# Hybrid RWKV-7 / HGRN2 step: norm_g spread earlier and by two engines, last masks moved to VectorE, one weight fetch moved up

## The chip, the cores and the metric

One core of one Trainium2 chip runs the kernel. The metric is device time in microseconds of one execution; before the change the median of 3 runs is 1124.75 us (1123.86 to 1125.27).

## The reference

One layer of a decoder trunk for 256 prompt tokens and 64 sample tokens (8 sequences of 8), all float32. Cut to what matters:

```
h = rms_norm(x, norm_g)                       # x * rsqrt(mean(x^2) + eps) * norm_g
p = h @ w_in                                  # one projection, 2048 -> P_TOTAL columns
cur = p[..., :SHIFT_W]; sh = cur + (prev - cur) * shift_mu
y_a, s_a = rwkv7_recurrence(r, decay, k, v, kk, a, s_a)   # S = S diag(w) - (S kk)(kk a)^T + v k^T
o_b, s_b = gla_chunkwise(q_b, k_b, i_b, log_g, s_b)       # S = diag(g) S + k v^T
merged = sigmoid(p_ga) * (y_a @ proj_a) + sigmoid(p_gb) * (y_b @ proj_b)
y = x + merged @ w_out; then a final rms_norm
```

Outputs are y for both groups and the new states.

## The kernel before, in words

The 320 tokens stand as columns. h is kept transposed and split into two parts (hhi and hlo, 16 blocks of 128 features); each block of 1024x128 weights is fetched into one of three raw buffers, split into whi (a cast by ScalarE) and wlo (a subtraction), and each output tile of 128 columns takes 16 x 3 products on TensorE (whi with hhi, whi with hlo, wlo with hhi), 48 of 320 columns in a row. After the opening a recorder (L69 to L292) lists the operations of the eight head pairs and a planner with costs orders them; that part and all that follows are not touched by the change.

The opening (L376 to L673) has two parts. Up to L497 the order is the program's own: loads on the sync queue, clearings and selections on GpSimd. Behind L544 the order of TensorE, ScalarE, VectorE and GpSimd is the order in which the code is written, so each engine's queue is first in, first out as the text stands.

What the opening does, with names. norm_g arrives as gq, four rows of 512. To spread it over 128 partitions it is split into two parts in gr (L574, L575), and four products with a selector sel write it to gps, from where it is copied to gb (L577 to L579). squares (L499) sums x squared per token on ScalarE, scale (L504) turns that into a factor ssq, gain (L510) multiplies x (xt) by ssq and gb on VectorE, in six instructions ahead of the first low part. turn (L520) transposes on TensorE into tps, high and low (L527, L531) make hhi and hlo. warm(n) (L539) puts n dummy products wps on TensorE, whose results nobody reads. first (L608) is the first output tile (wd, ad; its columns start at 128*24), worked off in pieces of four blocks; half (L615) splits half a weight block, with GpSimd subtracting; divide(2, 1, G) and divide(0, 1, G) (L398, L657, L668) split a whole block with GpSimd subtracting. fetch (L394) loads a block; fetch(2, 1024, 1) at L669 writes the raw buffer that divide(2, 1, G) has read, so it waits for that subtraction.

On GpSimd stand, ahead of those subtractions, the masks: mk (the third of three pairs, L473 to L475, is a product with seqm) and mu8, four copies of mf as bytes (L493, L494). Behind the first tile the transposes cps and sps give cols and sst (L658 to L664), from which bounds (L679) and wd_ad (L1374) make neg, lbt and uQ; uQ becomes lora_a and lora_w, and the product called a in the profile (a<-lora_a,ast) is the first on TensorE that needs them.

Of the kernel before, what the change touches and what calls it, by code (L numbers as in the profile page):

```python
# [9 lines left out]
F32 = mybir.dt.float32  # L10
# [284 lines left out]
def hybrid_step(ctx, tc, x_prompt, x_sample, state_rwkv, state_hgrn, state_shift, norm_g, w_in,  # L295
# [4 lines left out]
    V, S, G, T = nc.vector, nc.scalar, nc.gpsimd, nc.tensor  # L300

    S.add_instruction(mybir.InstLoadActFuncSet(
        name=nc.get_next_instruction_name(), act_func_set_id=EXP_LN_SET, ins=[], outs=[]))
# [11 lines left out]
    def ctile(shape, name, dt=F32, pool=rconst):  # L315
        return pool.tile(shape, dt, name=name, tag=name)
# [59 lines left out]
    with tc.tile_pool(name="start", bufs=1) as st, \  # L376
            tc.tile_pool(name="pst", bufs=6, space=PSUM) as pst:
        gq = st.tile([4, 512], F32, name="gq")
        nc.sync.dma_start(gq, norm_g.rearrange("o (r c) -> (o r) c", c=512))
        gb = st.tile([128, D], F32, name="gb")  # L380
# [13 lines left out]
        def fetch(b_, c0, k8):  # L394
            nc.sync.dma_start(wraw[b_], win[1024 * k8:1024 * k8 + 1024, c0:c0 + 128]
                              .rearrange("(k p) c -> p k c", p=128))

        def divide(b_, n, sub):  # L398
            for j in range(n):
                ks = slice(8 * j // n, 8 * (j + 1) // n)  # L400
                S.copy(whi[b_][:, ks], wraw[b_][:, ks])
                sub.tensor_sub(wlo[b_][:, ks], wraw[b_][:, ks], whi[b_][:, ks].bitcast(F32))
            return whi[b_], wlo[b_]

        for k8 in range(2):
            fetch(k8, 128 * 24, k8)

        gr = st.tile([64, 512], F32R, name="gr")
        sel = st.tile([64, 4, 128], F32R, name="sel")
# [13 lines left out]
        for r0, t_ in ((W0, w0), (A0, a0), (KK_, k_k), (KA, k_a), (LW, ln_w), (LB, ln_b), (LG, lb_logits)):  # L423
# [3 lines left out]
        ssr = st.tile([100, 2, 128], F32, name="ssr")  # L427
        nc.sync.dma_start(ssr, state_shift[0].rearrange("s (r c) -> (s r) c", c=128)
                          .rearrange("(j q) c -> q j c", j=2))
        fetch(2, 0, 0)  # L430


        id64 = ctile([128, 64], "id64")
        G.tensor_add(id64, ident[:, 0:64], ident[:, 64:128])
# [1 line left out]
        def keep_ge(ap, pattern, base, cm, fill=0.0):  # L436
            G.affine_select(out=ap, in_=ap, pattern=pattern, compare_op=ALU.is_ge, fill=fill,
                            base=base, channel_multiplier=cm)
# [8 lines left out]
        seqm = ctile([128, NSEQ], "seqm")  # L447
# [19 lines left out]
        mk = ctile([128, 3, 2, 64], "mk")  # L467
        G.memset(mk[:, 0:2], 1.0)
        for c_ in range(2):
            for sl in HS:  # L470
                keep_ge(mk[sl, c_], [[1, 2], [1, 64]], -1, -1)
        blk = seqm[:, :, None].to_broadcast([128, 8, 8])
        for x in range(2):  # L473
            G.tensor_mul(mk[:, 2, x].rearrange("p (s i) -> p s i", i=8),
                         mk[:, 0, x].rearrange("p (s i) -> p s i", i=8), blk)  # L475


        mf = st.tile([32, 3, 32], F32, name="mf")
        mu8 = ctile([128, 3, 32], "mu8", U8)
        G.memset(mf, 1.0)  # L480
        for n, sz in enumerate((8, 8, 16)):
# [8 lines left out]
            G.memset(lv[:, :, 0, :], 0.0)  # L490
            keep_ge(lv[:, :, 1, :], [[-2 * sz, nb], [0, sz]], 0, 1)
            keep_ge(lv[:, :, 1, :], [[2 * sz, nb], [0, sz]], sz - 1, -1)
        for g in range(4):  # L493
            G.tensor_copy(mu8[32 * g:32 * g + 32], mf)  # L494

        junk = st.tile([128, D], F32, name="junk")
        ssq = [st.tile([128, 2], F32, name=f"ssq{j}") for j in range(3)]  # L497

# [40 lines left out]
        def warm(n):  # L539
            for _ in range(n):  # L540
                T.matmul(wps[:, :256], ones[:, :128], ones, start=True, stop=True)

        tps = {}
        with tc.manual_schedule(engines={mybir.EngineType.PE, mybir.EngineType.Activation, mybir.EngineType.DVE,  # L544
                                        mybir.EngineType.Pool}):
            ones = st.tile([128, 256], F32R, name="ones")
            V.memset(ones.bitcast(F32), 1.0)

            jr_sum, jr_mean, jr_cent, jr_all = (ctile([128, 128], n, F32R)
                                                for n in ("jr_sum", "jr_mean", "jr_cent", "jr_all"))  # L550
            V.memset(jr_all.bitcast(F32), 1.0 / 128.0)
            for t_, x in ((jr_sum, 1.0), (jr_mean, 1.0 / 64.0)):
                V.memset(t_.bitcast(F32), 0.0)
                for sl in HS:
                    V.memset(t_[sl, sl].bitcast(F32), x)
            V.tensor_sub(jr_cent, ident, jr_mean.bitcast(F32))

            yz = ctile([128, 2, 2, 2, 64], "yz")
            yd = ctile([128, 2, 2, 64], "yd")
            qz = ctile([128, NSEQ, 32], "qz")  # L560
            arp = ctile([128, 5, 2, 2, 64], "arp")
            for t_ in (yz, qz, lora_lw[HS[1]].bitcast(F32), lora_la[HS[0]].bitcast(F32)):
                V.memset(t_, 0.0)


            rs_a = ctile([128, NT], "rs_a")
            rs_b = ctile([128, NT], "rs_b")
            V.memset(rs_a, 1.0)
            V.memset(rs_a[:, 0:NP_:64], 0.0)
            V.memset(rs_a[:, NP_::8], 0.0)  # L570
            V.memset(rs_b, 1.0)
            V.memset(rs_b[:, ::8], 0.0)

            S.copy(gr[0:4], gq)  # L574
            V.tensor_sub(gr[32:36], gq, gr[0:4].bitcast(F32))  # L575
            for c_ in range(4):
                ps = pst.tile([128, 512], F32, name="gps", tag="t")  # L577
                T.matmul(ps, sel[:, c_], gr, start=True, stop=True)
                V.tensor_copy(gb[:, 512 * c_:512 * c_ + 512], ps)  # L579
            V.memset(arp, 0.0)  # L580
            warm(16)
            squares(2)
            scale(2)
            gain(2, 0, 2)
            turn(2, 0)
            warm(3)
            gain(2, 2, 2)
            turn(2, 1)
            warm(4)
            squares(0)  # L590
            scale(0)
            gain(0, 0, 2)
            turn(0, 0)
            turn(0, 1)
            squares(1)
            scale(1)
            gain(0, 2, 2)
            gain(1, 0)
            turn(1, 0)
            gain(1, 1)  # L600
            turn(1, 1)
            high(2, 0)
            high(0, 0)
            low(2, 0)
            low(0, 0)
            first_ps = psm.tile([128, 512], F32, name="mps", tag="m")

            def first(part, k4):  # L608

                w, x = ((whi, hhi), (whi, hlo), (wlo, hhi))[part]  # L610
                for k_ in range(4 * k4, 4 * k4 + 4):
                    T.matmul(first_ps[:, :NT], w[k4 // 2][:, k_ % 8], x[:, k_], start=part == 0 and k_ == 0,
                             stop=part == 2 and k_ == KT - 1)

            def half(b_, hf):  # L615

                ks = slice(4 * hf, 4 * hf + 4)
                S.copy(whi[b_][:, ks], wraw[b_][:, ks])
                G.tensor_sub(wlo[b_][:, ks], wraw[b_][:, ks], whi[b_][:, ks].bitcast(F32))

            half(0, 0)
            high(1, 0)
            low(1, 0)
            first(0, 0)
            gain(1, 2)
            gain(1, 3)
            half(0, 1)
            high(2, 1)
            high(0, 1)
            high(1, 1)  # L630
            low(2, 1)
            low(0, 1)
            low(1, 1)
            turn(0, 2)
            first(0, 1)
            turn(1, 2)
            first(1, 0)
            first(2, 0)
            half(1, 0)
            high(0, 2)  # L640
            high(1, 2)
            low(0, 2)
            low(1, 2)
            turn(0, 3)
            turn(1, 3)
            first(0, 2)
            first(1, 1)
            first(2, 1)
            half(1, 1)
            fetch(0, 0, 1)  # L650
            high(0, 3)
            high(1, 3)
            low(0, 3)
            low(1, 3)
            first(1, 2)
            first(2, 2)
            divide(2, 1, G)  # L657
            ps = pst.tile([128, 512], F32, name="cps", tag="t")  # L658
            T.transpose(ps[:, :128], rows, ident)
            V.tensor_copy(cols, ps[:, :106])  # L660
            ps = pst.tile([128, 512], F32, name="sps", tag="t")
            for j in range(2):
                T.transpose(ps[:, 100 * j:100 * j + 100], ssr[:, j], ident[:100, :100])
            V.tensor_copy(sst.rearrange("p s r -> p (s r)"), ps[:, :200])  # L664
            for part in range(3):
                first(part, 3)
            fetch(1, 1024, 0)
            divide(0, 1, G)  # L668
            fetch(2, 1024, 1)  # L669
            for j in range(4):  # L670
                S.copy(seq4[32 * j:32 * j + 32], seqm[0:32, 0:4])
            S.copy(lvz[HS[1], :, 1], lvs[low_])
            S.copy(lvz[low_, :, 0], lvs[low_])  # L673
# [766 lines left out]
    with tc.manual_schedule():  # L1440
# [3 lines left out]
        V, S, G, T, Y = (book.proxy(e) for e in ("V", "S", "G", "PE", "Y"))  # L1444
        record_all()
        V, S, G, T = real
# [27 lines left out]
    for m in range(KT):  # L1474
# [7 lines left out]
        ps = psf.tile([128, 512], F32, name="ppa", tag="f")  # L1482
# [3 lines left out]
        ps = psf.tile([128, 512], F32, name="ppb", tag="f")  # L1486
# [143 lines left out]
```

## Time and profile before

| what | us |
|---|---|
| median of 3 runs | 1124.75 (1123.86 to 1125.27) |
| profiled execution, its own time | 1124.7 |
| its span in the trace | 1122.0 |
| TensorE busy | 1102.9 (98%) |
| VectorE busy | 760.4 (68%) |
| ScalarE busy | 693.2 (62%) |
| GpSimd busy | 192.8 (17%) |

The names in the profile are PE for TensorE (PEld its weight loads), DVE for VectorE, ACT for ScalarE, POOL for GpSimd and SPq for the sync queue. A time of a row is counted from the span's start. In a timeline, a row is one instruction or several alike in a run; the bracket is the engine's idle time before it and what ended that. The ends of matmuls are modelled and reach into the next row, and spans on GpSimd are rough. The granted clock is 1.0 in every slice of the opening.

### The profile page before, as it was taken

What the parts mean: (1) busy time and instruction counts of PE and PEld (TensorE: products, weight loads), DVE (VectorE), ACT (ScalarE), POOL (GpSimd) and SP (SyncE); (2) the same over time, 40 slices, a digit from 0 to 9 for tenths busy, and PEclk for the clock granted to TensorE, in tenths of its full rate; (3) what the DMA queues carried; (4) which work ended last, traced back from release to release, by engine and by line L of the source; (5) the groups of instructions that cost most, each with busy time, mean ns of one, the idle gap of its engine ahead of it and who ended that gap; (6) DMA issues with size and microseconds to landing.
All of it is one profiled execution on the core that took longest, in us unless ns stands there. A gap on an engine that the chain in (4) does not pass through costs nothing.

```text
span 1122.0 us, 23659 instructions
## 1 busy us (share of the span) xinstructions
PE 1102.9 (98%) x9240; PEld 1066.5 (95%) x9240; DVE 760.4 (68%) x1618; ACT 693.2 (62%) x1572; POOL 192.8 (17%) x411
## 2 busy tenths in 40 slices
PE   6999999999999999999999999999999999999997
PEld 5999999999999999999999999999999999988886
DVE  8778888887887887887887876444444444437532
ACT  6777777677778678677776876444444444436322
POOL 9531231221311411412312200000000000000000
PEclk9999999999999999999999999999999999999999
DMA  6743545435435436435444354555555555587512
GB/s 177 202 130 107 152 118 146 136 100 157 125 96 158 131 105 165 133 106 159 117 132 137 101 142 142 147 151 150 149 151 150 150 150 149 151 256 267 173 35 93
DMA packets 283107, 159.87 MB, mean 142 GB/s; under 512 B 22893, under 2 KB 273264, under 8 KB 282356
## 3 DMA queue, kind: packets, MB, share of 16 engines
q1 hardware_dynamic: 282996, 158.37, 49.5%
q8 instruction: 72, 1.18, 0.5%
q14 instruction: 39, 0.32, 0.1%
HBM read 148.53 MB, written 9.81 MB: 141 GB/s over the span
## 4 chain that ended last, share of the span: by engine, by line
PE 94%; POOL 2%; ACT 2%; issue 1%; DVE 0%; DMA 0%; ACTq 0%; POOLq 0%; DVEq 0%
PE mps L1448 41%; PE a L1448 10%; PE mps L359 6%; PE mps L360 6%; PE mps L361 6%; PE b L1448 3%; PE po L1531 3%; PE po L1533 3%; PE po L1532 3%; PE ppa L359 2%; PE ppb L360 2%; PE ppb L359 2%; PE ppa L360 2%; PE ppb L361 2%; PE ppa L361 2%; PE y L1448 1%
## 5 line engine op out<-in xcount | busy, mean ns | idle before, releaser
L1448 PE MATMUL mps<-hhi,whi 128*128 128x320 f32 x1088 | 345.1, 317 | 0.0
L1448 PE MATMUL mps<-hlo,whi 128*128 128x320 f32 x1088 | 344.6, 317 | 0.0
L1448 PE MATMUL mps<-hhi,wlo 128*128 128x320 f32 x1088 | 344.1, 316 | 0.0
L1448 PEld LDWEIGHTS mps<-hhi,whi 128*128 128x128 f32 x1088 | 205.0, 188 | 3.6 <-issue 2.7
L1448 PEld LDWEIGHTS mps<-hlo,whi 128*128 128x128 f32 x1088 | 205.1, 188 | 1.1 <-issue 0.4
L1448 PEld LDWEIGHTS mps<-hhi,wlo 128*128 128x128 f32 x1088 | 205.0, 188 | 0.7
L349 ACT CAST whi<-raw 128x1024 fp32r<-128x1024 f32 x88 | 92.4, 1050 | 162.7 <-PE mps L360 107.3
L350 DVE TENSOR_TENSOR wlo<-raw,whi 128x1024 fp32r<-128x1024 f32 x88 | 107.8, 1226 | 124.9 <-ACT whi L349 124.8
L1448 DVE TENSOR_TENSOR wlo<-raw,whi 128x1024 fp32r<-128x1024 f32 x134 | 164.7, 1229 | 17.1 <-ACT whi L1448 15.9
L1448 ACT CAST whi<-raw 128x1024 fp32r<-128x1024 f32 x134 | 140.2, 1046 | 57.0 <-PE mps L1448 54.6
L361 PE MATMUL mps<-hhi,wlo 128*128 128x320 f32 x448 | 138.7, 310 | 0.0
L359 PE MATMUL mps<-hhi,whi 128*128 128x320 f32 x448 | 138.7, 310 | 0.0
L360 PE MATMUL mps<-hlo,whi 128*128 128x320 f32 x448 | 138.7, 309 | 0.0
L361 PEld LDWEIGHTS mps<-hhi,wlo 128*128 128x128 f32 x448 | 84.1, 188 | 0.0
L360 PEld LDWEIGHTS mps<-hlo,whi 128*128 128x128 f32 x448 | 84.1, 188 | 0.0
L359 PEld LDWEIGHTS mps<-hhi,whi 128*128 128x128 f32 x448 | 84.1, 188 | 0.0
L1520 DVE TENSOR_TENSOR wlo<-raw,whi 128x1024 fp32r<-128x1024 f32 x32 | 38.6, 1223 | 39.0 <-ACT whi L1519 38.9
L1519 ACT CAST whi<-raw 128x1024 fp32r<-128x1024 f32 x32 | 33.0, 1050 | 48.5 <-DMA raw<-in_w_out_dram 21.3
L1448 POOL TENSOR_TENSOR vm<-v,seq 96x512 fp32r<-96x512 f32 x16 | 16.9, 1054 | 200.1 <-ACT uK L1448 152.4
L1531 PE MATMUL po<-whi,mhi 128*128 128x512 f32 x128 | 50.1, 392 | 0.7 <-DVE gbt L1488 0.7
L1533 PE MATMUL po<-wlo,mhi 128*128 128x512 f32 x128 | 50.1, 391 | 0.0
L1532 PE MATMUL po<-whi,mlo 128*128 128x512 f32 x128 | 50.0, 391 | 0.0
(435 smaller groups left out, 2244.0 us busy)
## 6 DMA issues: line engine op xcount, KB each, us to landing
raw<-in_w_in_dram SPq DMA_DIRECT2D x194, 512.0 KB
raw<-in_w_out_dram SPq DMA_DIRECT2D x32, 512.0 KB
raw<-in_proj_a_dram SPq DMA_DIRECT2D x16, 512.0 KB
raw<-in_proj_b_dram SPq DMA_DIRECT2D x16, 512.0 KB
s<-in_state_hgrn_dram SPq DMA_DIRECT2D x8, 512.0 KB
out_dram<-s SPq DMA_DIRECT2D x8, 512.0 KB
s<-in_state_rwkv_dram SPq DMA_DIRECT2D x8, 256.0 KB
out_dram<-s SPq DMA_DIRECT2D x8, 256.0 KB
```

Of the source, the lines that this page charges most:

```text
L349: S.copy(hi[:, ks], raw[:, ks])
L350: sub.tensor_sub(lo[:, ks], raw[:, ks], hi[:, ks].bitcast(F32))
L359: T.matmul(dst, hi[:, q, :], xhi[:, k, :], start=(k == 0), stop=False)
L360: T.matmul(dst, hi[:, q, :], xlo[:, k, :], start=False, stop=False)
L361: T.matmul(dst, lo[:, q, :], xhi[:, k, :], start=False, stop=(k == nk - 1))
L1448: o.fn(*o.args, **o.kw)
L1519: S.copy(hi, raw)
L1520: V.tensor_sub(lo, raw, hi.bitcast(F32))
L1531: T.matmul(pt, h, hi, start=first, stop=False)
L1532: T.matmul(pt, l, hi, start=False, stop=False)
L1533: T.matmul(pt, h, lo, start=False, stop=end)
```

## The change

The split of norm_g and its four products move ahead of VectorE's clearings of yz, qz and the others; of the four copies to gb ScalarE makes the first and third. The dummy products ahead of the first transpose grow from 16 to 20. The product that makes the last pair of mk and the four copies of mu8 leave GpSimd and stand on VectorE behind divide(2, 1, G), ahead of the copy to cols. The fetch of the third weight block is issued ahead of the small loads.

```diff
--- before.py
+++ after.py
@@ -404,6 +404,7 @@
 
         for k8 in range(2):
             fetch(k8, 128 * 24, k8)
+        fetch(2, 0, 0)
 
         gr = st.tile([64, 512], F32R, name="gr")
         sel = st.tile([64, 4, 128], F32R, name="sel")
@@ -427,8 +428,6 @@
         ssr = st.tile([100, 2, 128], F32, name="ssr")
         nc.sync.dma_start(ssr, state_shift[0].rearrange("s (r c) -> (s r) c", c=128)
                           .rearrange("(j q) c -> q j c", j=2))
-        fetch(2, 0, 0)
-
 
         id64 = ctile([128, 64], "id64")
         G.tensor_add(id64, ident[:, 0:64], ident[:, 64:128])
@@ -469,10 +468,6 @@
         for c_ in range(2):
             for sl in HS:
                 keep_ge(mk[sl, c_], [[1, 2], [1, 64]], -1, -1)
-        blk = seqm[:, :, None].to_broadcast([128, 8, 8])
-        for x in range(2):
-            G.tensor_mul(mk[:, 2, x].rearrange("p (s i) -> p s i", i=8),
-                         mk[:, 0, x].rearrange("p (s i) -> p s i", i=8), blk)
 
 
         mf = st.tile([32, 3, 32], F32, name="mf")
@@ -490,9 +485,6 @@
             G.memset(lv[:, :, 0, :], 0.0)
             keep_ge(lv[:, :, 1, :], [[-2 * sz, nb], [0, sz]], 0, 1)
             keep_ge(lv[:, :, 1, :], [[2 * sz, nb], [0, sz]], sz - 1, -1)
-        for g in range(4):
-            G.tensor_copy(mu8[32 * g:32 * g + 32], mf)
-
         junk = st.tile([128, D], F32, name="junk")
         ssq = [st.tile([128, 2], F32, name=f"ssq{j}") for j in range(3)]
 
@@ -555,6 +547,13 @@
                     V.memset(t_[sl, sl].bitcast(F32), x)
             V.tensor_sub(jr_cent, ident, jr_mean.bitcast(F32))
 
+            S.copy(gr[0:4], gq)
+            V.tensor_sub(gr[32:36], gq, gr[0:4].bitcast(F32))
+            for c_ in range(4):
+                ps = pst.tile([128, 512], F32, name="gps", tag="t")
+                T.matmul(ps, sel[:, c_], gr, start=True, stop=True)
+                (V.tensor_copy if c_ % 2 else S.copy)(gb[:, 512 * c_:512 * c_ + 512], ps)
+
             yz = ctile([128, 2, 2, 2, 64], "yz")
             yd = ctile([128, 2, 2, 64], "yd")
             qz = ctile([128, NSEQ, 32], "qz")
@@ -570,15 +569,8 @@
             V.memset(rs_a[:, NP_::8], 0.0)
             V.memset(rs_b, 1.0)
             V.memset(rs_b[:, ::8], 0.0)
-
-            S.copy(gr[0:4], gq)
-            V.tensor_sub(gr[32:36], gq, gr[0:4].bitcast(F32))
-            for c_ in range(4):
-                ps = pst.tile([128, 512], F32, name="gps", tag="t")
-                T.matmul(ps, sel[:, c_], gr, start=True, stop=True)
-                V.tensor_copy(gb[:, 512 * c_:512 * c_ + 512], ps)
             V.memset(arp, 0.0)
-            warm(16)
+            warm(20)
             squares(2)
             scale(2)
             gain(2, 0, 2)
@@ -655,6 +647,12 @@
             first(1, 2)
             first(2, 2)
             divide(2, 1, G)
+            blk = seqm[:, :, None].to_broadcast([128, 8, 8])
+            for x in range(2):
+                V.tensor_mul(mk[:, 2, x].rearrange("p (s i) -> p s i", i=8),
+                             mk[:, 0, x].rearrange("p (s i) -> p s i", i=8), blk)
+            for g in range(4):
+                V.tensor_copy(mu8[32 * g:32 * g + 32], mf)
             ps = pst.tile([128, 512], F32, name="cps", tag="t")
             T.transpose(ps[:, :128], rows, ident)
             V.tensor_copy(cols, ps[:, :106])
```

VectorE's queue in the opening, before, from the first clearing of yz to that of arp:

```order
L563 MEMSET yz 128x512
L563 MEMSET qz 128x256
L563 MEMSET lora_lw 64x320
L563 MEMSET lora_la 64x320
L568 MEMSET rs_a 128x320
L569 MEMSET rs_a 128x4
L570 MEMSET rs_a 128x8
L571 MEMSET rs_b 128x320
L572 MEMSET rs_b 128x40
L575 TENSOR_TENSOR gr<-gq,gr 4x512
L579 COPY gb<-gps 128x512 x4
L580 MEMSET arp 128x1280
```

And in the changed kernel, over the same stretch:

```order
L551 TENSOR_TENSOR gr<-gq,gr 4x512
L555 COPY gb<-gps 128x512 x2
L562 MEMSET yz 128x512
L562 MEMSET qz 128x256
L562 MEMSET lora_lw 64x320
L562 MEMSET lora_la 64x320
L567 MEMSET rs_a 128x320
L568 MEMSET rs_a 128x4
L569 MEMSET rs_a 128x8
L570 MEMSET rs_b 128x320
L571 MEMSET rs_b 128x40
L572 MEMSET arp 128x1280
```

gr and gb stand ahead of all clearings, and two of the four copies are gone from this queue.

ScalarE's queue at its start, before (gq and gr as above, xt is x, of which number 103 is x_sample):

```order
L302 ACT_TABLE_LOAD
L574 CAST gr<-gq 4x512
L502 ACTIVATE junk,ssq_196<-xt_103 64x2048
L507 ACTIVATE ssq_196<-ssq_196,eps_n 64x1
L508 ACTIVATE ssq_196<-ssq_196 64x1
```

And changed:

```order
L302 ACT_TABLE_LOAD
L550 CAST gr<-gq 4x512
L555 COPY gb<-gps 128x512 x2
L494 ACTIVATE junk,ssq_190<-xt_103 64x2048
L499 ACTIVATE ssq_190<-ssq_190,eps_n 64x1
L500 ACTIVATE ssq_190<-ssq_190 64x1
```

The two copies to gb stand between the cast to gr and the first squares.

VectorE's queue behind the first tile, before, from the last low parts (hlo) to lbt:

```order
L533 TENSOR_TENSOR hlo<-tps,hhi 128x4x128 x6
L660 COPY cols<-cps 128x106
L664 COPY sst<-sps 128x200
L1448 TENSOR_SCALAR neg<-cols 128x16
L1448 TENSOR_TENSOR lbt<-cols 128x8
L1448 RECIPROCAL lbt<-lbt 128x8
```

And changed:

```order
L525 TENSOR_TENSOR hlo<-tps,hhi 128x4x128 x6
L652 TENSOR_TENSOR mk<-mk,seqm 128x64 x2
L655 CAST mu_176<-mf 32x96 x4
L658 COPY cols<-cps 128x106
L662 COPY sst<-sps 128x200
L1446 TENSOR_SCALAR neg<-cols 128x16
L1446 TENSOR_TENSOR lbt<-cols 128x8
L1446 RECIPROCAL lbt<-lbt 128x8
```

Six instructions now stand between the last low part and cols, and all behind them is queued behind the six.

## Rows read from the trace of the kernel before

**Rows 1.** The page, busy time of the engines (us, share, instructions)

```profile
PE 1102.9 (98%) x9240; PEld 1066.5 (95%) x9240; DVE 760.4 (68%) x1618; ACT 693.2 (62%) x1572; POOL 192.8 (17%) x411
```

**Rows 2.** Waits of TensorE from 40 us to the end (engine, line, releaser, times, longest)

```profile
PE a L1448 <- DVE pp L1448: 0.7, 2, 0.3
PE po L1531 <- DVE gbt L1488: 0.7, 1, 0.7
```

**Rows 3.** Timeline of TensorE, opening (start us, us, what, pause before and its end)

```profile
6.76 2.04 PE L578 MATMUL gps<-gr,sel 64*128 64x512 f32 x4 [6.76 <-DVE gr L575]
8.73 3.78 PE L541 MATMUL wps<-ones 128*128 128x256 f32 x16
...
16.89 1.32 PE L525 MATMUL tps<-ident,xt 128*128 128x128 f32 x8 [0.85 <-DVE xt L513]
...
22.48 0.85 PE L612 MATMUL mps<-hhi,wlo 128*128 128x320 f32 x4 [0.41 <-POOL wlo L619]
23.18 1.03 PE L525 MATMUL tps<-ident,xt 128*128 128x128 f32 x8
...
38.12 0.39 PE L1448 MATMUL a<-lora_a,ast 128*128 128x320 f32 x1 [0.85 <-DVE ast L1448]
```

**Rows 4.** Timeline of VectorE, opening

```profile
2.52 0.68 DVE L556 TENSOR_TENSOR jr_cent<-ident,jr_mean 128x128 fp32r<-128x128 f32 x1
...
5.93 0.68 DVE L575 TENSOR_TENSOR gr<-gq,gr 4x512 fp32r<-4x512 f32 x1
7.56 2.49 DVE L579 COPY gb<-gps 128x512 f32<-128x512 f32 x4 [0.95 <-PE gps L578]
10.26 1.12 DVE L580 MEMSET arp<- 128x1280 f32 x1 [0.21 <-issue]
11.30 6.19 DVE L513 SCALAR_TENSOR_TENSOR xt<-xt,ssq,gb 64x1024 f32<-64x1024 f32 x6
```

**Rows 5.** Timeline of ScalarE, opening

```profile
6.64 1.91 ACT L502 ACTIVATE junk<-xt 64x2048 f32<-64x2048 f32 x1 [3.54 <-DMA xt<-in_x_sample_dram]
...
24.77 1.06 ACT L401 CAST whi<-raw 128x1024 fp32r<-128x1024 f32 x1
27.80 1.05 ACT L401 CAST whi<-raw 128x1024 fp32r<-128x1024 f32 x1 [1.97 <-DMA raw<-in_w_in_dram]
...
33.17 1.05 ACT L1448 CAST whi<-raw 128x1024 fp32r<-128x1024 f32 x1 [1.38 <-DMA raw<-in_w_in_dram]
```

**Rows 6.** Timeline of GpSimd, opening

```profile
10.02 6.27 POOL L474 TENSOR_TENSOR mk<-mk,seqm 128x64 f32<-128x64 f32 x2
...
21.14 5.04 POOL L619 TENSOR_TENSOR wlo<-raw,whi 128x512 fp32r<-128x512 f32 x4
26.12 2.41 POOL L402 TENSOR_TENSOR wlo<-raw,whi 128x1024 fp32r<-128x1024 f32 x1
28.93 2.42 POOL L402 TENSOR_TENSOR wlo<-raw,whi 128x1024 fp32r<-128x1024 f32 x1 [0.39 <-ACT whi L401]
```

**Rows 7.** Timeline of VectorE behind the first tile

```profile
27.29 0.27 DVE L660 COPY cols<-cps 128x106 f32<-128x106 f32 x1 [1.57 <-PE cps L659]
...
27.75 0.82 DVE L1448 TENSOR_SCALAR neg<-cols 128x16 f32<-128x16 f32 x1
...
33.50 0.70 DVE L1448 SCALAR_TENSOR_TENSOR uQ<-dif,cols,pad 128x256 f32<-128x256 f32 x2
```

**Rows 8.** VectorE groups by form (count, busy us, mean ns of one, idle)

```profile
L1448 DVE CAST fq<-f 32x8 fp32r<-32x8 f32 x32 | 6.9, 215 | 0.4
...
L1493 DVE TENSOR_TENSOR ms<-mt,ms 128x64 fp32r<-128x64 f32 x16 | 3.5, 219 | 0.0
```

**Rows 9.** Timeline of the sync queue, two fetches of weight blocks

```profile
23.70 0.39 SPq L395 DMA_DIRECT2D raw<-in_w_in_dram  x1
...
28.56 0.37 SPq L395 DMA_DIRECT2D raw<-in_w_in_dram  x1
```

## Prediction

> **What bounds the kernel now.** I read the shares of the engines first. TensorE is busy for 1102.9 of 1122.0 us [rows 1], so the end moves only by what moves TensorE. Next I read whom TensorE waits for behind 40 us: 0.7 us for pp and 0.7 us for po, nothing else [rows 2]. So an earlier TensorE at 40 us is an earlier end by as much, and all that matters lies ahead of 40 us. There the TensorE timeline is the view to read, with what ended each pause in brackets [rows 3]: it starts at 6.76 when VectorE has made gr, fills time with dummy products (wps), waits 0.85 us for the scaled input (xt) at 16.89, 0.41 us at 22.48 for GpSimd's wlo, and 0.85 us at 38.12 for VectorE's ast. Between 22.48 and the wait at 38.12 it has no pause. So there are two limits one behind the other: the first transposes and products, and the chain that ends in the product "a" at 38.12. A gain in the first is kept only if the second comes earlier too.
>
> **The first limit: the spread of norm_g.** VectorE's queue before [rows 4]: jr_cent ends at 3.20, then memsets to 5.93 (2.73 us), gr 5.93 to 6.61, a wait for the four gps products, four copies to 10.05, the arp memset, and from 11.30 the six gains (xt), which run to 17.49 without a pause. The change puts gr right behind jr_cent: 3.26 + 0.68 = 3.94. The gps products began 0.15 us behind gr (6.61 to 6.76), so now at 4.09; as before the first can be copied 0.80 later (6.76 to 7.56) and the last ends 2.04 after the start, 6.13, the third about 0.43 earlier, 5.70. ScalarE's two copies, at VectorE's 0.62 each (2.49 / 4), end at 5.51 and 6.32; ScalarE has nothing to do until x_sample lands at 6.64 [rows 5], so they cost it nothing, with 0.3 us to spare. VectorE's second copy is 6.17 to 6.79. Then the same memsets (2.73) and the stretch from the end of the copies to the first gain (10.05 to 11.30, 1.25, or 1.04 without the short pause ahead of arp): gains from 10.56 to 10.77 instead of 11.30. The squares that they need are ready by then, since ScalarE's work is not moved. That is 0.53 to 0.74 us; I take 0.6. TensorE waits for these gains at 16.89, so its transposes come 0.6 us earlier, and ScalarE's casts behind them. The four more dummy products take 4 x 0.236 us (3.78 / 16); with the start 2.67 us earlier they end near 10.5 to 10.8, ahead of the first transpose near 11.9, so they cost nothing.
>
> **GpSimd's relief.** The two mk products took 6.27 us on GpSimd, though they are tiny: they stood against the gains [rows 6], and the four mu casts stood behind them. Without them GpSimd is at its first subtract when ScalarE has cast the half block, and not at 21.14. So the 0.41 us pause at 22.48 goes. A group's modelled end reaches past the start of the next one (22.48 + 0.85 = 23.33, against 23.18 [rows 3]), so what goes is the 0.41 and 0.15 to 0.24 of such an overlap: 0.6. The late wait there is then ScalarE's chain of casts, which is 0.6 earlier already. Together TensorE's turn at 23.18 comes 1.2 us earlier. What could take from that: a half-block subtract on GpSimd (5.04 / 4 = 1.26 us) can now fall between two gains and push the second. Below that costs nothing, where ScalarE's casts hide it; above, I put it at 0.5 us. I take nothing.
>
> The third block's fetch moves ahead of eleven small loads on the sync queue. ScalarE did not wait for that block at 24.77 [rows 5], so it gains nothing; the small loads are needed only by the transposes ahead of cols at 27.29 [rows 7], and slip by the one issue. Nothing either way.
>
> **The second limit: the masks behind the first tile.** They now stand on VectorE between its last low part (hlo) and cols. Nothing on VectorE pays directly: it idled 1.57 us there, from 25.72 to 27.29 [rows 7]. The six instructions have near rows of 0.219 (128x64) and 0.215 (a cast of 32 partitions) [rows 8]; I take 2 x 0.22 + 4 x 0.20 = 1.24. But GpSimd wants to start its whole-block subtract in the same moment, when ScalarE's cast ends, 24.77 + 1.06 = 25.83 [rows 5]. The trace shows that such instructions of the two engines exclude each other: the two mk products above, and VectorE's tiny neg, which took 0.82 us and ended as the subtract did, 26.12 + 2.41 = 28.53 [rows 6, 7]. All times 1.2 earlier: masks 24.52 to 25.76, subtract asked for at 24.63 and started at 25.80, so it waits about 1.15. It ends at 28.21 instead of 28.53: the relief at this place is 0.32, not 1.2. Its wait is between 0.1 (it gets in behind the first mask) and 1.4 (casts of 0.26).
>
> Two chains hang on it. First the fetch of the next block: issued at 28.56 behind the subtract, and ScalarE's cast of it begins at 33.17, 4.61 later; the one issued at 23.70 was cast at 27.80, 4.10 later [rows 5, 9]. The earlier fetches now lie further ahead, so I take the middle, 4.36: 28.24 + 4.36 = 32.60, cast to 33.65, against 34.23. Second, VectorE: its operations behind neg wait for the second subtract (28.93 + 2.42 = 31.35), and it needs 2.85 from there to the end of uQ (33.50 + 0.70 = 34.20). The second subtract now follows the first with neg between them: 28.25 + 0.15 + 2.42 = 30.8, so uQ is done at 33.65. Both chains meet there; ScalarE's uQ can start 0.58 earlier than at 34.23. From there to "a" it is 3.89 (34.23 to 38.12), so "a" comes at 37.54. TensorE arrives 1.2 earlier, at 36.07 instead of 37.27, and waits 1.47 us instead of 0.85.
>
> **Sum.** Opening -1.2, growth of the wait at "a" +0.62: -0.6. The profiled execution took 1124.7 us (span 1122.0 and 2.7 around it), 0.05 under the median of 1124.75: 1124.1. Bounds from the unknown terms: GpSimd's wait of 0.1 with a landing of 4.10 gives a gain of 1.6; a wait of 1.4, a landing of 4.61 and the 0.5 for a pushed gain give +0.1 to +0.3.
>
> A rule that bears on this: the Trainium skill, SBUF — State Buffer, section "SBUF: two separate sides", states that VectorE and GpSimd share one pair of ports, which the instruction that starts first holds whole while the other blocks. The trace agrees that they block each other; but two mk products waited through four gains, so at half of the ends of an instruction VectorE went on. By the rule read strictly, in turns of one instruction, GpSimd would get in behind the first mask, and the time would be that of the second rival.
>
> **Rivals.**
> 1. The relief comes through: GpSimd gets the pair early, VectorE's masks still fit into the 1.57 us that it idled, and the fetch lands in 4.10. Then the subtract ends at 27.15, the next cast begins at 31.28, the second subtract ends at 29.75 and uQ at 32.6: 1.6 earlier than 34.23, so 1123.1. For it: GpSimd got in at two of four such places. Against it: the masks are short and queued back to back, and start a tenth before the subtract is asked for. If the opening gains more (0.74 and 0.65) it reaches 1122.6.
> 2. GpSimd gets in twice: behind the first mask, and again behind the second. Then the four casts stand behind its second subtract: 24.52 + 0.22 + 2.41 + 0.22 + 2.42 = 29.8, casts to 30.6, cols, sst and neg to 31.4 instead of 28.6. ScalarE's lbt stands ahead of two casts of 1.05 each, the first of which ends at 32.8; VectorE's wlo, dif and uQ behind it take 2.4 and end at 35.2, 1.0 later than 34.20: 1125.7, slower than before. It decides from the point where uQ's end passes 34.20, that is, when cols starts later than about 29.6. For it: the two engines in turns, as the rule has it. Against: VectorE kept the pair past half of the ends, and the casts are perhaps free of it.
> 3. The idle time on TensorE between the dummy products and the first transpose grows from none to 1.1 to 1.4 us, and the products before it run in 0.236 us each, at the low of the two clock levels, which TensorE left only near the end of the 16 [rows 3]. If it has not left that level, or falls back to it, transposes and first products take twice as long: eight transposes took 1.03 us at 23.18, so the four that ScalarE's next cast waits for cost 0.5 more, and products up to 22 us some 1.7 on top (two groups of 0.85, doubled). The time is then 1124.6 to 1126. Against it: behind the pause of 0.41 at 22.48 the transposes kept their pace.
>
> **How the numbers follow.** Forecast 0.52 (1123.4 to 1124.8), rival 1 0.23, rival 2 0.13, rival 3 0.12. A measurement of this kernel can tell about 0.2%, 2.25 us, from no change: faster means below 1122.5, slower above 1127.0. Only the far end of rival 1 is below: 0.08. Only the far ends of rivals 2 and 3 together are above: 0.04. The rest, 0.88, is no change that can be told. The range leaves out a tenth on each side: 1122.5 to 1125.8.
>
> **What would show it.** Right: gps starts near 4.1, the first gain near 10.6, no wait of TensorE for GpSimd's wlo at 22, GpSimd's first whole-block subtract about 1 us behind ScalarE's cast, and the wait for ast grown to about 1.5 us. Wrong: gains still from 11.3; masks on VectorE stretched to over 2 us (rival 2); the wait for ast at 0.85 or less with an earlier fetch (rival 1); transposes of over 0.2 us behind 12 us (rival 3); or any new wait of TensorE behind 40 us.

## The result and the profile after

The changed kernel took 1126.28 us (median of 22 runs, 1124.92 to 1128.36) against 1124.36 us (22 runs, 1123.65 to 1125.27): ratio 1.0016, 95% interval [1.001, 1.0022]. It is 1.9 us slower, where 0.6 us faster was forecast; the median lies beyond the upper end of the range, though still within the 0.2% that counted as no change. The profiled execution took 1125.44 us with a span of 1123.7; that of before 1124.7 with 1122.0. Some 1.7 us lie around the span in most profiled executions here, 2.7 in that of before, so spans are compared.

First TensorE's pauses from 40 us on, whom it waited for and for how long in all; they answer to [rows 2].

```profile
PE a L1446 <- DVE pp L1446: 0.7, 2, 0.3
PE po L1529 <- DVE gbt L1486: 0.7, 1, 0.7
PE b L1446 <- DVE k L1446: 0.2, 1, 0.2
```

Besides 0.2 us for k nothing is new there: the time was lost ahead of 40 us. TensorE's timeline, the rows that answer to [rows 3]:

```profile
4.44 2.04 PE L554 MATMUL gps<-gr,sel 64*128 64x512 f32 x4 [4.44 <-DVE gr L551]
6.42 4.63 PE L533 MATMUL wps<-ones 128*128 128x256 f32 x20
12.36 0.71 PE L517 MATMUL tps<-ident,xt 64*128 64x64 f32 x8 [1.31 <-DVE xt L505]
...
22.14 0.75 PE L604 MATMUL mps<-hhi,wlo 128*128 128x320 f32 x4
22.72 1.26 PE L517 MATMUL tps<-ident,xt 128*128 128x128 f32 x8
...
39.44 0.39 PE L1446 MATMUL a<-lora_a,ast 128*128 128x320 f32 x1 [2.16 <-DVE ast L1446]
```

The wait at 22 us is gone and the turn at 23.18 comes at 22.72, so 0.46 of the 1.2 us arrived there. But TensorE reaches its wait for ast at 39.44 - 2.16 = 37.28, before at 38.12 - 0.85 = 37.27: nothing of the opening's gain is left. And the wait is 2.16 instead of 0.85, so "a" is 1.32 us later, of a span that grew by 1.7. The other 0.4 lie behind 40 us; 0.2 of them is the wait for k, the rest is not settled by this trace. VectorE, to be held against [rows 4, 7]:

```profile
3.24 1.06 DVE L551 TENSOR_TENSOR gr<-gq,gr 4x512 fp32r<-4x512 f32 x1
...
11.15 6.06 DVE L505 SCALAR_TENSOR_TENSOR xt<-xt,ssq,gb 64x1024 f32<-64x1024 f32 x6
...
18.94 3.74 DVE L505 SCALAR_TENSOR_TENSOR xt<-xt,ssq,gb 128x512 f32<-128x512 f32 x2
22.60 4.26 DVE L525 TENSOR_TENSOR hlo<-tps,hhi 128x512 fp32r<-128x512 f32 x7
26.78 3.71 DVE L652 TENSOR_TENSOR mk<-mk,seqm 128x64 f32<-128x64 f32 x2
30.41 0.83 DVE L655 CAST mu<-mf 32x96 uint8<-32x96 f32 x4
31.28 0.27 DVE L658 COPY cols<-cps 128x106 f32<-128x106 f32 x1
...
34.96 0.70 DVE L1446 SCALAR_TENSOR_TENSOR uQ<-dif,cols,pad 128x256 f32<-128x256 f32 x2
```

and GpSimd, against [rows 6]:

```profile
3.84 0.64 POOL L433 TENSOR_TENSOR id<-ident 128x64 f32<-128x64 f32 x1
...
9.89 6.07 POOL L436 TENSOR_SCALAR_AFFINE_SELECT mf<-mf 32x32 f32<-32x32 f32 x1
...
17.92 4.20 POOL L611 TENSOR_TENSOR wlo<-raw,whi 128x512 fp32r<-128x512 f32 x3
22.94 1.28 POOL L611 TENSOR_TENSOR wlo<-raw,whi 128x512 fp32r<-128x512 f32 x1 [0.81 <-ACT whi L610]
25.63 4.78 POOL L402 TENSOR_TENSOR wlo<-raw,whi 128x1024 fp32r<-128x1024 f32 x2 [1.41 <-ACT whi L401]
```

In the place of the two mk products a small selection into mf now takes 6.07 us; before it stood behind them and was quick:

```profile
16.25 0.66 POOL L437 TENSOR_SCALAR_AFFINE_SELECT mf<-mf 32x32 f32<-32x32 f32 x1
```

Then read the two engines side by side. The two mk products, 128x64 each, take 3.71 us on VectorE while GpSimd's two whole-block subtractions run back to back from 25.63 to 30.41. The view of the tile mk tells the two apart (shortest/median/longest, in ns):

```profile
L652 DVE TENSOR_TENSOR mk<-mk,seqm x2: 1330/1892/2455, 26.8 to 28.0; 128x64 f32<-128x64 f32 x2
```

The first stood 1.33 us until the first subtraction was through, the second 2.46 us, the whole of the second one. So cols is at 31.28 instead of 27.29, and uQ starts at 34.96 instead of 33.50. On ScalarE a second thing shows:

```profile
31.40 0.38 ACT L1446 COPY pad<-mps 128x256 f32<-128x256 f32 x1 [3.52 <-issue]
...
35.70 0.47 ACT L1446 ACTIVATE uQ<-uQ 64x320 f32<-64x320 f32 x1 [1.49 <-DVE uQ L1446]
```

ScalarE idled 3.52 us ahead of its first copy into pad, which reads nothing that the masks make, and the idle time ends just behind the last cast of mu.

### The profile page after: what moved, and what is told of

It is laid out like the page before. It is cut to its first block, busy times and chain, and to the rows that moved or that the text cites. A ratio compares the mean times of both kernels' runs of the same rounds, so it can differ in the third digit from the quotient of the medians.

```text
span 1123.7 us, 23670 instructions
## 1 busy us (share of the span) xinstructions
PE 1104.4 (98%) x9244; PEld 1067.0 (95%) x9244; DVE 765.0 (68%) x1622; ACT 694.7 (62%) x1574; POOL 191.0 (17%) x405
## 4 chain that ended last, share of the span: by engine, by line
PE 95%; ACT 2%; DVE 1%; issue 1%; POOL 0%; ACTq 0%; DVEq 0%; POOLq 0%
PE mps L1446 42%; PE a L1446 10%; PE mps L360 6%; PE mps L361 6%; PE mps L359 6%; PE b L1446 3%; PE po L1531 3%; PE po L1529 3%; PE po L1530 3%; PE ppb L360 2%; PE ppa L360 2%; PE ppb L361 2%; PE ppb L359 2%; PE ppa L361 2%; PE ppa L359 2%; PE y L1446 1%
```

## The experiments

Every kernel was timed in five rounds, beside the kernel before in the same rounds, whose medians were 1124.01, 1124.41, 1123.90 and 1124.01 us in the four sets. "The six mask lines" are the two lines of blk, the loop over mk and the loop over mu8, as in the change.

**First set: the parts (before: 1124.01).** masks_back is the change without its masks part.

```diff
-            [the six mask lines on V behind divide(2, 1, G)]
+        [the six mask lines on G, where the kernel before has them]
```

> The changed kernel with only the masks put back on GpSimd, where they were; the early spread of norm_g, 20 dummy products and the early fetch stay. Theory P (the port): the loss is that VectorE's two mk products wait for GpSimd's two whole-block subtractions and cols comes 4 us late. Then TensorE's wait for ast falls from 2.16 us to about 0.9, VectorE's gains stay near 11.2, and the executions that are not touched by the clock take about 1124.2, 0.2 under before. Theory C (the clock): the loss is that TensorE idles between the dummies and the first transpose, and in a part of the executions the first transposes and products run at 1.2 GHz. Then the spread between executions stays at about 3 us here, with a part near 1126 to 1127, and the median stays 1 us or more above before.

1123.20 us (1122.61 to 1124.33), ratio 0.999 [0.9981, 0.9998]: faster than before, by 0.8 us. masks_alone is the other half: the kernel before with nothing but the six lines moved to VectorE.

> The kernel before with only the masks moved to VectorE behind the first tile; norm_g, dummies and fetch as before. Theory P: TensorE's wait for ast grows to about 2 us and the time is about 1125.2, 0.8 over before, with all executions within about 1.6 us of each other, as before. Theory C: nothing of the idle time is changed, so 1124.4 and no spread beyond that of before.

1126.69 us (1125.08 to 1128.50), ratio 1.0018 [1.001, 1.0026]. The masks part alone makes the whole loss (1.0016 with all parts). Its executions stood in two groups, 5 at 1125.1 to 1125.4 and 6 at 1126.7 to 1127.3, and one at 1128.50, which is the profiled one. In its windows the figure in question is the granted clock, behind the five busy times:

```profile
40.00:41.00 1.00, 1.00 (x7) 1.00 (x6) 0.92 (x3) 1.00 (x2) 1.00 (x5) 0.72 1.21 295
41.00:42.00 1.00, 1.00 (x5) 0.96 (x5) 0.57 (x1) 1.00 (x3) 0.89 (x5) 0.50 1.20 291
42.00:43.00 1.00, 1.00 (x7) 1.00 (x6) 0.65 (x1) 1.00 (x4) 1.00 (x4) 0.50 0.50 114
43.00:44.00 1.00, 1.00 (x6) 1.00 (x6) 0.70 (x1) 0.97 (x4) 0.23 (x2) 0.57 0.17 27
```

TensorE waited 2.17 us for ast there, until 39.25; about 1.2 us later it stands at the lower level, 1.2 GHz, from some 40.44 to 43.86 (0.72 and 0.57 of these two windows), and its products follow one another in 0.27 instead of 0.147 us:

```profile
39.25 0.38 PE L1448 MATMUL a<-lora_a,ast 128*128 128x320 f32 x1 [2.17 <-DVE ast L1448]
...
40.06 0.31 PE L1448 MATMUL mps<-hlo,whi 128*128 128x320 f32 x1
40.20 0.31 PE L1448 MATMUL mps<-hhi,wlo 128*128 128x320 f32 x1
...
42.71 0.47 PE L1448 MATMUL mps<-hlo,whi 128*128 128x320 f32 x1
42.98 0.47 PE L1448 MATMUL mps<-hhi,wlo 128*128 128x320 f32 x1
```

3.4 us at half speed are 1.7 us of work lost. This profiled execution lies beyond the second group as well, by 1.5 us of span; two pauses of TensorE of 0.9 and 0.7 us late in the kernel, which the kernel before does not have, make that up. In the changed kernel's own profiled execution, one of its faster ones, the level stays full from 12 us to the last microseconds. fill_28 fills the new idle time ahead of the first transpose.

```diff
-            warm(20)
+            warm(28)
```

> The changed kernel with 28 dummy products instead of 20, so that TensorE has work up to about 12.3 us at the lower clock, where it idled from 10.85 to 12.36. Theory C: the executions above 1126 go, and the median falls from 1126.3 to about 1125.2. Theory P: the wait for ast is unchanged at about 2.2 us, so 0.8 over before remains; by P alone the spread of the changed kernel would have another cause and the median would stay at 1126.3.

1126.57 us (1124.89 to 1127.01), ratio 1.0015 [1.0007, 1.0023]: no better in the median. But 8 of the changed kernel's 22 executions lay at 1127.06 to 1128.36, and none of the 12 here: 4 at 1124.9 to 1125.1, 8 at 1126.3 to 1127.0. masks_late leaves the masks on GpSimd, behind its last whole-block subtraction.

```diff
             divide(2, 1, G)
-            [the six mask lines, on V]
...
             divide(0, 1, G)
+            [the six mask lines, on G]
```

> The changed kernel with the masks on GpSimd, but behind its last whole-block subtraction. Theory P: VectorE's queue is free, cols comes at about 27.3, the wait for ast is 1 us or less, and the quiet executions take about 1124. If instead the early subtractions of GpSimd collide with VectorE's gains (third theory, G: the second pair of gains took 3.74 us instead of 1.39), TensorE reaches the second tile no earlier than before and the gain of the opening is lost here too: first tile done at about 29.2, as before, and the quiet executions at about 1124.4. Theory C: a part of the executions is still near 1126 or above.

1127.16 us (1125.23 to 1127.87), ratio 1.0025 [1.0016, 1.0034]: a miss, and the useful one. VectorE is free, and yet "a" comes later still, behind a wait of 2.85 us (rows of its timeline). The granted clock behind that wait, unlike in masks_alone, stays at 1.00:

```profile
26.83 4.79 POOL L402 TENSOR_TENSOR wlo<-raw,whi 128x1024 fp32r<-128x1024 f32 x2 [1.23 <-ACT whi L401]
...
28.20 0.27 DVE L652 COPY cols<-cps 128x106 f32<-128x106 f32 x1 [1.19 <-PE cps L651]
...
31.57 0.55 POOL L663 TENSOR_TENSOR mk<-mk,seqm 128x64 f32<-128x64 f32 x2
...
32.07 1.17 POOL L666 CAST mu<-mf 32x96 uint8<-32x96 f32 x4
...
33.27 0.38 ACT L1446 COPY pad<-mps 128x256 f32<-128x256 f32 x1 [4.21 <-POOL mu L666]
...
41.04 0.39 PE L1446 MATMUL a<-lora_a,ast 128*128 128x320 f32 x1 [2.85 <-DVE ast L1446]
```

pad waits 4.21 us for the mu casts, though it uses nothing of theirs. It is the memory: mf lies in the opening's pool (start), and pad is laid into what that pool frees, so its first write waits for mf's last reader.

**Second set: which of the two holds the chain (before: 1124.41).** Theory P is the one of the two engines that exclude each other, M the one of the memory. mf_kept is the changed kernel with mf in memory that outlives the pool (in the tile sga, which is written much later and is laid out earlier in the program for this).

```diff
-        mf = st.tile([32, 3, 32], F32, name="mf")
+        mf = sga[:32, 0, :96].rearrange("p (n i) -> p n i", n=3)
```

> The changed kernel, masks on VectorE, but mf lies in memory that is not given up with the opening's pool (in sga, which is written much later). Theory M (memory): the tile pad reuses the memory of the opening's pool, so ScalarE's first copy to pad waits for the last reader of mf, the mu casts, and that wait (3.52 us, to 31.40) is the loss. Then pad comes at about 29.3, TensorE's wait for ast is 1 us or less, and the median is about 1124. Theory P (queue and port): cols stands behind the masks on VectorE, which stand behind GpSimd's two subtractions, and that alone makes uQ late. Then pad is early, but cols still at about 31.3, the wait for ast still 2.2 us, the median still 1125 to 1126.6. If both hold one beside the other, this is as by P.

1127.21 us (1124.87 to 1129.07), ratio 1.0021 [1.0012, 1.003]. pad is early now, and nothing is won:

```profile
26.20 4.78 POOL L403 TENSOR_TENSOR wlo<-raw,whi 128x1024 fp32r<-128x1024 f32 x2 [1.22 <-ACT whi L402]
...
26.34 4.72 DVE L653 TENSOR_TENSOR mk<-mk,seqm 128x64 f32<-128x64 f32 x2
...
29.57 0.38 ACT L1446 COPY pad<-mps 128x256 f32<-128x256 f32 x1 [1.15 <-issue]
...
31.85 0.27 DVE L659 COPY cols<-cps 128x106 f32<-128x106 f32 x1
...
40.02 0.38 PE L1446 MATMUL a<-lora_a,ast 128*128 128x320 f32 x1 [2.46 <-DVE ast L1446]
```

P alone is enough. mf_kept_late is masks_late with the same line.

> Masks on GpSimd behind its last whole-block subtraction, as in masks_late, and mf in memory that is not given up. Theory M: ScalarE's copy to pad comes at about 29.5 to 30 instead of 33.27; what is left is GpSimd's own small copy to pad, which stands behind the masks at about 33.3, so uQ ends near 35 instead of 37.3, the wait for ast falls from 2.85 to about 1 us, and the median is 1124 to 1125. Without M (pad late for another reason): as masks_late, 1127.2.

1124.70 us (1123.74 to 1126.19), ratio 1.0001 [0.9992, 1.001]: against its sibling masks_late (1.0025) that is 2.7 us, by the ratios (in the two profiles "a" stands at 41.04 and at 39.31, 1.7 us apart; what made the rest is not shown). So M is real as well; in the changed kernel it lies beside P, in the same microseconds. masks_in_gap then puts the masks where both leave room: on GpSimd, ahead of its first whole-block subtraction.

```diff
             half(1, 1)
+            [the six mask lines, on G]
             fetch(0, 0, 1)
...
             divide(2, 1, G)
-            [the six mask lines, on V]
```

> The changed kernel with the masks on GpSimd between its fourth half-block subtraction and the first whole-block one, where it idled 1.41 us. By M and P both: mf is read out by about 26, cols is not held up, the first whole-block subtraction slips by about 0.3 us; the wait for ast is below 1 us, no execution loses 1.6 us to the clock behind that wait, and the median is 1123 to 1123.7, as or under that of masks_back (1123.2).

1123.96 us (1122.88 to 1124.89), ratio 0.9994 [0.9986, 1.0003]. The loss is gone: the masks take 1.7 us there, cols is at 26.78.

```profile
24.11 0.56 POOL L644 TENSOR_TENSOR mk<-mk,seqm 128x64 f32<-128x64 f32 x2
...
24.61 1.16 POOL L647 CAST mu<-mf 32x96 uint8<-32x96 f32 x4
...
25.85 4.78 POOL L402 TENSOR_TENSOR wlo<-raw,whi 128x1024 fp32r<-128x1024 f32 x2
...
26.78 0.27 DVE L658 COPY cols<-cps 128x106 f32<-128x106 f32 x1 [1.11 <-PE cps L657]
```

norm_only is masks_back with the fetch where the kernel before has it.

> masks_back with the third weight block's fetch back behind the small loads, so only the spread of norm_g and the 20 dummies are left of the change. If the gain of masks_back (0.8 us) is the spread's, this takes about 1123.2; if it is the fetch's (the later fetches find the queue free and ScalarE no longer waits 1.97 us for a block at 27.8), it takes about 1124.

1124.08 us (1122.64 to 1125.32), ratio 0.9996 [0.9987, 1.0005]. Its profiled execution, the slowest of them, waits for a VectorE subtraction late in the kernel, which the kernel before does not:

```profile
PE po L1532 <- DVE wlo L1519: 1.2, 1, 1.2
```

**Third set: the clock in the opening, and the fetch (before: 1123.90).** In masks_back the granted clock was at half behind the idle time ahead of the first transpose, 1.85 us (its windows; the clock is the figure ahead of the last two):

```profile
12.00:14.00 2.00, 1.63 (x12) 1.34 (x13) 2.00 (x3) 1.97 (x3) 2.00 (x3) 0.79 1.21 291
14.00:16.00 2.00, 2.00 (x13) 1.88 (x14) 2.00 (x3) 1.11 (x5) 2.00 (x3) 0.50 1.21 290
16.00:18.00 2.00, 2.00 (x11) 2.00 (x10) 2.00 (x4) 1.00 (x2) 2.00 (x7) 0.50 0.39 91
18.00:20.00 2.00, 2.00 (x10) 1.78 (x9) 1.17 (x3) 1.40 (x4) 1.72 (x6) 0.51 0.18 54
```

back_fill28 and gap_fill28 are masks_back and masks_in_gap with warm(28); fetch_alone is the kernel before with the third block's fetch moved up alone.

> The change without its masks part (as masks_back, 1123.20), with 28 instead of 20 dummy products ahead of the first transpose. C (clock): masks_back's profile had the clock at half from 13.14 to 19.97 us; filled, it stays at full level, the first transposed tile comes 0.3 to 0.8 us earlier, and the median is 1122.5 to 1123.0. N (hidden): 1123.0 to 1123.4, as masks_back. Both theories: no wait ahead of a over 0.9 us.

1123.39 us (1123.32 to 1123.87), ratio 0.9994 [0.9985, 1.0003]. The level stayed full, the times lie closer together, but the median did not come down: with the masks early on GpSimd the half level in the opening costs nothing that could be measured, as theory N had it.

> The masks on GpSimd between its fourth half-block subtraction and its first whole-block one, as in masks_in_gap (1123.96, span 1121.2 in its profile), and with 28 instead of 20 dummy products ahead of the first transpose. Two theories on the time left in masks_in_gap. C (TensorE's clock): its profile shows the clock at half from 14.87 to 18.28 us, behind the idle stretch ahead of the first transpose at 12.37; with the stretch filled the clock stays at full level in every execution, the first transposed tile is ready earlier, and the median comes to 1122.9 to 1123.3, under 1124.0 in nearly all executions. N (the half-level stretch in the opening is hidden by waits on other engines, and the spread of the times has another cause): the median stays at 1123.7 to 1124.3 with the same spread. The wait for ast ahead of the product a stays under 0.9 us by both.

1122.93 us (1122.63 to 1123.84), ratio 0.9989 [0.998, 0.9998], as theory C had it: 1.0 us faster than before, and the executions of masks_in_gap at 1124.1 to 1124.9 have no counterpart. The intervals of the two kernels overlap, though, so how much the fill adds to masks_in_gap is not settled. TensorE no longer waits for ast:

```profile
37.15 0.39 PE L1446 MATMUL a<-lora_a,ast 128*128 128x320 f32 x1
```

> The kernel before with the third weight block's fetch moved up alone; norm, clearings and masks as before. F (the fetch is what sets masks_back at 1123.20 apart from norm_only at 1124.08): 0.5 to 0.9 us faster than before. G (the fetch brings nothing, as predicted; norm_only is pulled up by its clock): within 0.2% of before, 1123.9 to 1124.8, and the wait on the whole-block subtraction ahead of po that norm_only shows is not in it.

1123.92 us (1123.10 to 1125.24), ratio 0.9998 [0.9989, 1.0007]: the fetch brings nothing by itself.

**Fourth set: the clock behind the wait (before: 1124.01).** fill_a is fill_28 with 14 dummy products ahead of "a".

```diff
+        gap = 14
         for o in book.order():
+            if gap and o.eng == "PE" and o.args[2].tensor.name.startswith("lora_a"):
+                while gap:
+                    T.matmul(o.args[0], jr_all, hhi[:, 0, :], start=True, stop=True)
+                    gap -= 1
             o.fn(*o.args, **o.kw)
```

> fill_28 (1126.57; its executions stood in two groups, 4 at 1124.9 to 1125.1 and 8 at 1126.3 to 1127.0) with 14 further dummy products of 128x320 just ahead of the first product a, into the memory that a then overwrites, so that TensorE works through most of its 2.2 us wait for ast and nothing comes later. Two theories on the slower group. C (clock): it is TensorE falling to half speed right behind that wait, as the profiles of masks_alone and mf_kept show it; with the wait filled the clock stays at full level, the wait ahead of a shrinks to about 0.1 us with a still at 39.3, and nearly all executions come at 1124.9 to 1125.4. D (the groups come from something else, such as a late fetch): the two groups remain, the median stays at 1126.3 to 1126.8. The direct part of the loss, about 1.0 to 1.3 us against the kernel before's wait of 0.85, is left in both.

1125.06 us (1124.59 to 1125.47), ratio 1.0009 [1.0, 1.0018]. The wait is filled, "a" is where it was, and all 11 executions stand in what was the faster group.

```profile
37.13 2.21 PE L1449 MATMUL a<-hhi,jr_all 128*128 128x320 f32 x14
39.36 0.41 PE L1451 MATMUL a<-lora_a,ast 128*128 128x320 f32 x1
```

So the loss of fill_28 splits: 1.05 us come from the longer wait itself, and 1.5 more in the median of fill_28 (1126.57 - 1125.06) from the clock that falls behind it, by the groups in 8 of 12 executions.

## Why the prediction was wrong

**gr and the copies: the mechanism right, the size off.** gr ran where it was forecast but took 1.06 instead of 0.68 us. It overlaps GpSimd's selections into sel (to 3.76) and its id addition (from 3.84, 0.64 us instead of 0.32), which the working did not look at; which of the two held it is not shown. Its end at 4.30 instead of 3.94 passes on: gps at 4.44 instead of 4.09, VectorE's last copy through at 7.22 instead of 6.79, gains from 11.15. The term of 0.6 us measured 0.15.

**GpSimd's relief: smaller than forecast.** "Without them GpSimd is at its first subtract when ScalarE has cast the half block" did not come true: the cast ended at 16.55, the subtract began at 17.92. The 6.27 us were not a matter of the mk products. The next instruction in the queue, the selection into mf, stood nearly as long in the same place. TensorE's wait at 22 us went all the same.

**A pushed gain.** GpSimd began its half-block subtractions at 17.92 instead of 21.14 [rows 6], and the next two gains took 3.74 us, before 1.39:

```profile
19.22 1.39 DVE L513 SCALAR_TENSOR_TENSOR xt<-xt,ssq,gb 128x512 f32<-128x512 f32 x2
```

The prediction had priced this and left it out: "Below that costs nothing, where ScalarE's casts hide it; above, I put it at 0.5 us. I take nothing". It measured some 2.3 us on VectorE. Its low parts then run without a pause from 22.60 and end only at 26.86, before at 25.72. TensorE reached "a" no sooner than before, though one wait had gone.

**The step that failed: "masks 24.52 to 25.76, subtract asked for at 24.63 and started at 25.80".** The order of the two was decided by a tenth of a microsecond, and by the pushed gain, taken at nothing, and the smaller gain at gr it turned round: the subtraction started at 25.63, the masks could not before 26.78. From there it is the second rival. The time forecast for it was 1125.7, cols, sst and neg to 31.4, uQ to 35.2; measured were 1126.28, neg to 31.91 and uQ to 35.66. The prediction had this rival at 0.13 because VectorE had kept the pair of ports past half of the ends of an instruction. In this place that did not hold: a subtraction, one mk product, the next subtraction, the next mk product, in turns. The Trainium skill (SBUF — State Buffer, "SBUF: two separate sides") states that whichever starts first has the shared pair of ports for the whole instruction and the other blocks; this trace agrees, with mk products of 1.33 and 2.46 us that end as the subtractions do. The casts, 0.83 for four, were near the 0.80 taken for them.

**What was not seen at all: the memory.** The working asked what is queued behind the masks, and not which memory their input holds. In the changed kernel that lies beside the first cause and adds nothing that could be measured (mf_kept); with the masks late on GpSimd it is the cause (masks_late against mf_kept_late, 2.7 us).

**The clock: right in kind, the place missed.** The third rival looked for it in the opening. It read the low level off the pace of the dummy products, 0.236 us each; the granted clock of that stretch reads 1.00, so their pace alone does not show it. It does fall there in some executions: fill_28 takes away the group above 1127.06, and the profile of mf_kept, at 1127.63 in that kernel's upper group, has a granted clock of 0.50 both in the opening (14 to 20 us) and behind "a" (41 to 44 us). The fall behind "a" no rival had, and it is 1.5 us in the median of fill_28: the prediction took the wait's growth as its whole price. No profile of the changed kernel's own slower executions was taken. Their mean granted clocks fit in the main, 0.993 to 0.995 in the eight above 1127 against 0.996 and 0.997 in the nine up to 1125.96. Of the five between, at 1126.10 to 1126.32, two have 0.999, the highest of all 22, so what made these slower stays open.

**What held.** The wait for wlo at 22 us went. The fetch brought nothing, though the small loads slipped by 3.3 us (the first is issued at 11.63, before at 8.29) and not "by the one issue"; nobody waited for them. Norm and fetch together (masks_back) gained 0.8 us [0.2, 2.1]; back_fill28, with the same parts and a longer fill, comes to 0.9994 with an interval that takes in no change, so the size is weakly known. What sets masks_back apart from norm_only (0.9990 and 0.9996, with intervals that overlap) stays open.

## What to carry to other kernels

When an instruction is moved to another engine, look up what the two engines that share a resource will run at its new place, and do not let the sign of the answer hang on a tenth of a microsecond in a start that you have estimated: masks of 1.2 us of work cost 4.5 us of VectorE's time against a neighbour's subtractions, and 1.7 us on the neighbour itself just ahead of them. A long row beside the other engine's work may be the place's and not the instruction's: the next one in the queue inherits the wait. Ask also which memory the moved instruction's input keeps from being used again. And price a longer pause of TensorE with the slow stretch that may follow it: a few dummy products in the pause tell the two apart, and here they are free.

## What the runs showed of the hardware

- A pause of 2.17 us of TensorE in the midst of dense products was followed in masks_alone by 3.4 us at 1.2 GHz, beginning 1.2 us behind the pause and not at it; by the groups of the times this was so in 8 of fill_28's 12 executions. It is not so each time: pauses of 2.16 us (after) and 2.85 us (masks_late) at the same place were not followed by it in their profiles, nor were those of 0.85 and 0.89 us (before, back_fill28). Products in the pause whose results nobody reads took the slower group away.
- The same half level in the opening (from some 13.1 to nearly 20 us in masks_back, by its windows) cost nothing that could be measured where other engines were late anyway.
- A 128x64 product of VectorE can take 2.46 us while GpSimd subtracts a whole block, and a 32x32 selection of GpSimd 6.07 us while VectorE clears arp and scales the input (0.66 behind that stretch in the kernel before).
